# A two-block transformer kernel: masked scores in SBUF, early gate and up products in pairs, other step counts around the second mix

## The chip, the cores and the metric

The kernel runs on one core of a Trainium2 chip. The metric is the device time of one launch in microseconds: 2547.01 us, the median of three runs (2543.77 to 2547.75).

## The reference

Two transformer blocks over 1024 rows of width 1024, all in 32-bit floats. Block one puts 16 meta rows ahead of the sequence, projects, and runs two mixers side by side: a differential attention of 4 heads and a state-space mixer. Block two has a gated spatial mixer and an attention of 8 heads with a forgetting bias. Both end with an output projection ("mix"), norms, and a feed-forward of hidden width 2816.

```python
def probs(qb, k):                                   # block one, per head and block of 128 queries
    s = jnp.einsum('bhqd,bhkd->bhqk', qb, k) * scale
    return jax.nn.softmax(jnp.where(causal, s, -jnp.inf), axis=-1)
attn = probs(q1b, k1) - lam * probs(q2b, k2)
out = jnp.einsum('bhqk,bhkd->bhqd', attn, v32)
...
mix = jnp.einsum('blc,cd->bld', jnp.concatenate([o, y], axis=-1), w_out[l])
h_res = h_res + rms_norm(mix, post_mix_g[l])
h = rms_norm(h_res, pre_ffn_g[l])
f = jax.nn.silu(h @ w_gate) * (h @ w_up)            # written as einsums
h_res = h_res + rms_norm(f @ w_down, post_ffn_g[l])
```

Block two's attention adds differences of a running sum of log gates to the scores and applies the softmax of each half-head by itself.

## The kernel before

**Number format.** A factor of a large product is kept as two rounded tiles, "hi" and "lo" (ScalarE copies into hi, VectorE or GpSimd subtracts for lo), and a product is three matmuls (`mm3`, `mma`: hi*hi, hi*lo, lo*hi). `wpiece` (L99) loads 512 KB of a weight (`wr`, a ring of 2) and splits it into `wh` and `wl`, rings of 4.

**Stages.** The sequence is worked on in two halves of 512 rows. Per block: dense projections, attention of the first half with the other mixer beside it, then `feed_forward` (L1234): the first half's mix (`mix_first`), its norms into H0 (`norm_first`), `up_first` and `down_sums` beside the second half's attention, the second half's mix and norms (`mix_second`, `norm_second`), then `ffn_up` and `ffn_down`, which multiply in a Strassen-like scheme. `up_first` makes those gate and up products that need H0 alone: for each of 11 tiles t of the hidden width one "half" of 24 matmuls for gate and one for up. Within a half, 12 matmuls give a partial product that ScalarE copies out (`p1`, L1038) and SyncE stores; 12 more then accumulate onto the same bank. Gate banks come from a pool of one (`psum_e`), up banks from a pool of two (`psum_d`). ScalarE applies Silu to the gate bank (L1041), VectorE multiplies the up bank in (L1043). `down_sums` (L1008) loads 1 MB of the down weight into a single buffer, forms four sums on GpSimd (L954) and stores them, 11 times.

**Attention.** A step takes one head and 128 queries. For each of the two q/k pairs (block one) or half-heads (block two), `scores` (L630) makes the score product in PSUM (`s`: two banks of 512 columns in the first half, one tile of two banks in the second; in block one, for the last of a half's four query blocks, a further short piece for the 16 meta columns in `t`), lets VectorE add the mask or bias and take the row minimum in one instruction that writes back to PSUM (L649, shown as CUSTOM_DVE_ANT_0 with an accumulator read), and lets ScalarE apply the exponential of each piece from PSUM into P in SBUF with the row sum (L656). Where there are two pieces, VectorE joins minima (L654) and sums (L659). P comes from a ring of four tiles that also holds the k tile of a head (`rowp`). In block one VectorE then combines both P (L754). `transposed_product` (L674) transposes P on TensorE in groups of four 128-column blocks, copies each group out of PSUM alternately on ScalarE (L626) and VectorE (L628), and multiplies with v. At a head's end the normalized output `ob` is stored to DRAM; the second mix loads it as `cat`.

**What sets the order.** The pieces are Python generators that are stepped in turn, which gives program order; a planner then orders every engine's instructions, and SyncE's DMA list, by program order and its own estimates of when inputs are ready. `ahead(n)` moves what is issued under it n instructions forward in priority. `pinned` (L110) ties the first matmul of an early product behind the last score or mix matmul issued before it (`mark`). Engines and SyncE's list run strictly in the order that the planner gave them.

Of the kernel before, what the change touches and what calls it, by code (L numbers as in the profile page):

```python
# [10 lines left out]
F32 = mybir.dt.float32  # L11
F32R = mybir.dt.float32r
I32 = mybir.dt.int32
AF = mybir.ActivationFunctionType
ALU = mybir.AluOpType
# [40 lines left out]
def tile_two_blocks(ctx: ExitStack, tc: tile.TileContext, a, out):  # L56
    nc = tc.nc
    PE, V, S, G, SP = nc.tensor, nc.vector, nc.scalar, nc.gpsimd, nc.sync
# [33 lines left out]
    fD = [dram.tile([7, NT, 128, 512], F32, name=f"fD{i}") for i in range(2)]  # L92
# [167 lines left out]
    def step(gen, n=1):  # L260
        for _ in range(n):
            next(gen, None)

    def ahead(n=500):
        return tc.high_priority(offset=n)
# [28 lines left out]
    with ExitStack() as pre:  # L294
        np_ = pool(pre, "p1n", 3, side="right")
        for rt in range(9):
            n = 128 if rt else NM
# [322 lines left out]

    turn = [0]

    def evac(out_, in_):
        turn[0] += 1
        if turn[0] % 2:
            S.activation(out=out_, in_=in_, func=AF.Copy)  # L626
        else:
            V.tensor_copy(out=out_, in_=in_)  # L628

    def scores(q, k, n, bias, nm, ls, P, fix=None):  # L630

        cuts = ([(0, 1, n)] if n <= 512 else [(0, 1, NM), (NM, 1, 512)] if n <= NH else
                [(0, 2, n // 2)] if n <= 1024 else [(0, 1, NM), (NM, 2, 512)])
        tiles = []
        if len(cuts) > 1:
            m2 = small.tile([128, 2], F32, tag="m2", name="m2")
        for ci, (c0, nb, w) in enumerate(cuts):
            s_ = (psum_s[0] if ci == len(cuts) - 1 else psum_t)()
            s_ = s_.rearrange("p (b c) -> p b c", c=512)
            for b in range(nb):  # L640
                for o in range(2):
                    i = PE.matmul(out=s_[:, b, 0:w], lhsT=q[:, o], rhs=k[:, c0 + b * w:c0 + (b + 1) * w],  # L642
                                  start=o == 0, stop=o == 1)
            sv = s_[:, 0:nb, 0:w]
            if fix is not None:
                dv = s_[:, nb - 1, w - 128:w]
                V.tensor_tensor(out=dv, in0=dv, in1=fix, op=ALU.add)
            bv = bias[:, c0:c0 + nb * w].rearrange("p (b c) -> p b c", b=nb)
            V.tensor_tensor_reduce(out=sv, in0=sv, in1=bv, scale=1.0, scalar=0.0, op0=ALU.add, op1=ALU.min,  # L649
                                   accum_out=m2[:, ci:ci + 1] if len(cuts) > 1 else nm)  # L650
            tiles.append((sv, c0, nb, w))
        mark[0] = i
        if len(cuts) > 1:
            V.tensor_tensor(out=nm, in0=m2[:, 0:1], in1=m2[:, 1:2], op=ALU.min)  # L654
        for ci, (sv, c0, nb, w) in enumerate(tiles):
            S.activation(out=P[:, c0:c0 + nb * w].rearrange("p (b c) -> p b c", b=nb), in_=sv, func=AF.Exp,  # L656
                         scale=-1.0, bias=nm, accum_out=ls[:, ci:ci + 1])
        if len(cuts) > 1:
            V.tensor_tensor(out=ls[:, 0:1], in0=ls[:, 0:1], in1=ls[:, 1:2], op=ALU.add)  # L659

    def split_pair(src, dst, o, eng, other=None):

# [8 lines left out]
                S.activation(out=dst[po, 1 - o, e], in_=src[pi], func=AF.Copy)  # L671
                eng[e].tensor_tensor(out=dst[pi, 1 - o, e], in0=src[pi], in1=hi.bitcast(F32), op=ALU.subtract)

    def transposed_product(bank, out_, P, blocks, last):  # L674

        for b0 in range(0, len(blocks), 4):
            grp = blocks[b0:b0 + 4]
            t = psum_t()
            at = atp.tile([128, 512], F32, tag="at", name="at")
            for b, (c0, w, _) in enumerate(grp):  # L680
                PE.transpose(out=t[0:w, b * 128:(b + 1) * 128], in_=P[:, c0:c0 + w], identity=ident)
            nb = sum(w == 128 for _, w, _ in grp)
            evac(at[:, 0:nb * 128], t[:, 0:nb * 128]) if nb else None
            for b, (c0, w, v) in enumerate(grp):
                if w < 128:
                    evac(at[0:w, b * 128:(b + 1) * 128], t[0:w, b * 128:(b + 1) * 128])
                bank.mm(out_, at[0:w, b * 128:(b + 1) * 128], v, last and b0 + b == len(blocks) - 1)

    def attention(blk, half, side, keep=None):
# [4 lines left out]
        with ExitStack() as ph:  # L694
# [39 lines left out]
            for h in range(4):  # L734
# [7 lines left out]
                for j in range(4):  # L742
                    i = half * 4 + j
                    n = m + (i + 1) * 128
                    P = [rowp.tile([128, nk], F32, tag="row", name="P") for _ in range(2)]
                    for e in range(2):
                        scores(qst[:, :, e, j * 128:(j + 1) * 128], kst[:, e], n,
                               mask[:, nk - n:nk] if blk == 0 else x[:, e, 0:n],
                               nm[:, j, e:e + 1], ls_[:, j, e], P[e], None if blk == 0 else mask)
                    V.reciprocal(out=rl[:, j], in_=ls_[:, j, :, 0])  # L750
                    if blk == 0:
                        V.tensor_scalar(out=cf[:, j:j + 1], in0=rl[:, j, 1:2], scalar1=ls_[:, j, 0, 0:1],
                                        scalar2=nlam[:, 0:1], op0=ALU.mult, op1=ALU.mult)
                        V.scalar_tensor_tensor(out=P[0][:, 0:n], in0=P[1][:, 0:n], scalar=cf[:, j:j + 1],  # L754
                                               in1=P[0][:, 0:n], op0=ALU.mult, op1=ALU.add)
                        blocks = [(NM + b * 128, 128, v[:, b]) for b in range(i + 1)] + [(0, NM, x)]
                        transposed_product(bank, o[:, j * 128:(j + 1) * 128], P[0], blocks, j == 3)
                    else:
                        for e in range(2):
                            es = slice(e * 64, (e + 1) * 64)  # L760
                            transposed_product(bank, o[:, j * 128 + e * 64:j * 128 + (e + 1) * 64], P[e],
                                               [(b * 128, 128, v[:, b, es]) for b in range(i + 1)], j == 3 and e == 1)
                    if j == 1 and h < 3:
                        nxt = load(h + 1)
                    yield
# [257 lines left out]
    def up_first(blk, H0):  # L1023

        sfx = "_2" if blk else ""
        for t in range(NT):
            f11 = rows_out.tile([128, 512], F32, tag="vt", name="f11")
            for g in range(2):
                u = wpiece(a[("w_up" if g else "w_gate") + sfx][t][:, 2:4].rearrange("p b k f -> p (b k f)"))
                bank = (psum_d if g else psum_e)()  # L1030
                for blkn, q in ((1, 0), (0, 1)):
                    for kt in range(4):
                        k0 = blkn * 512 + kt * 128
                        mma(bank, sl(u, slice(None), slice(k0, k0 + 128)), sl(H0, slice(None), 4 * q + kt),
                            q == 0 and kt == 0, q == 0 and kt == 0)
                    if q == 0:
                        s = rows_out.tile([128, 512], F32, tag="vt", name="p1")
                        S.activation(out=s, in_=bank, func=AF.Copy)  # L1038
                        SP.dma_start(out=pD[blk][2 * t + g], in_=s)
                if g == 0:  # L1040
                    S.activation(out=f11, in_=bank, func=AF.Silu)  # L1041
                else:
                    V.tensor_tensor(out=f11, in0=f11, in1=bank, op=ALU.mult)  # L1043
                    SP.dma_start(out=fD[blk][0, t], in_=f11)
                yield

    def ffn_up(blk, A, raws):

# [185 lines left out]
    def feed_forward(blk, att, ffs, fp, mT):  # L1234

        _, _, _, gains = ffn_args(blk)
        with ffs:
# [16 lines left out]
            upf = up_first(blk, H0)  # L1254
            with ExitStack() as th:
                ds = down_sums(blk, pool(th, "utd", 1, side="right"))
                for n in (2, 2, 1, 2, 2, 1, 2, 2, 2):
                    step(att)
                    step(upf, n)
                    step(ds)  # L1260
                drain(ds)
                drain(att)
# [8 lines left out]
            with ExitStack() as mh:  # L1271
                mp = pool(mh, "mx", 2)
                tp = pool(mh, "mxt", 3)
                gp = row_bcast(mp, gains[0], 1024, "ffg0", 1)
                gT = mp.tile([128, KT], F32, name="ffgT", bufs=1)
                SP.dma_start(out=gT, in_=a["ffn_gT_2" if blk else "ffn_gT"])
                ms = mix_second(blk, mp, lambda rt, xt: norm_second(blk, mp, tp, gp, gT, rt, H0, A, F, xt))
                for n in (1, 0, 0, 0, 0, 0, 1):
                    with ahead(400):
                        step(ms)  # L1280
                    step(upf, n)
                for _ in range(2):
                    with ahead(400):
                        step(ms)
                    step(upf, 2)
                drain(ms)
                drain(upf)
            for n, x, q in (("S3", F[0], 0), ("S4", F[1], 1)):
# [316 lines left out]
```

## Time and profile before

| | us |
|---|---|
| median of 3 runs | 2547.01 |
| the profiled execution, its own time | 2551.87 |
| its span in the trace | 2550.2 |
| TensorE busy (share of the span) | 2335.1 (92%) |
| VectorE | 1548.2 (61%) |
| ScalarE | 1131.9 (44%) |
| GpSimd | 869.7 (34%) |
| mean granted TensorE clock | 0.962 |

PE is TensorE's matmul row and PEld its weight loads, DVE is VectorE, ACT ScalarE, POOL GpSimd, SP SyncE (SPq its list of DMAs). Busy time leaves out waiting. The granted clock is the share of full speed; 1.0 is 2.4 GHz. Attention beside other work lies at about 180 to 680 us (block one) and 1400 to 1890 (block two), the second mixes at about 700 to 820 and 1914 to 2030, the large feed-forward products between and after.

### The profile page before, as it was taken

What the parts mean: (1) busy time and instruction counts of PE and PEld (TensorE: products, weight loads), DVE (VectorE), ACT (ScalarE), POOL (GpSimd) and SP (SyncE); (2) the same over time, 40 slices, a digit from 0 to 9 for tenths busy, and PEclk for the clock granted to TensorE, in tenths of its full rate; (3) what the DMA queues carried; (4) which work ended last, traced back from release to release, by engine and by line L of the source; (5) the groups of instructions that cost most, each with busy time, mean ns of one, the idle gap of its engine ahead of it and who ended that gap; (6) DMA issues with size and microseconds to landing.
All of it is one profiled execution on the core that took longest, in us unless ns stands there. A gap on an engine that the chain in (4) does not pass through costs nothing. (4 is left out here: it accounts for less than half of the span.)

```text
span 2550.2 us, 31792 instructions
## 1 busy us (share of the span) xinstructions
PE 2335.1 (92%) x11016; PEld 1891.9 (74%) x11016; DVE 1548.2 (61%) x2485; ACT 1131.9 (44%) x1962; POOL 869.7 (34%) x690
## 2 busy tenths in 40 slices
PE   8997799679698999989999999998979899999997
PEld 6765678567576888868887778877867688887886
DVE  8658764765357667654586446556436776665556
ACT  4334544455354322325454566456535422223543
POOL 1747321134424666620002121113442466661001
PEclk9998989789899999999999999999999999999999
DMA  4432225246764454556666222644676454545666
GB/s 162 145 120 76 72 74 167 90 151 221 259 207 137 159 172 153 173 162 200 196 231 203 80 75 94 224 141 142 226 257 242 150 166 167 169 162 195 207 195 213
DMA packets 201409, 422.83 MB, mean 166 GB/s; under 512 B 33752, under 2 KB 52312, under 8 KB 195104
## 3 DMA queue, kind: packets, MB, share of 16 engines
q1 hardware_dynamic: 201248, 420.79, 49.9%
q8 instruction: 87, 1.43, 0.2%
q14 instruction: 74, 0.61, 0.1%
HBM read 308.78 MB, written 110.76 MB: 165 GB/s over the span
## 5 line engine op out<-in xcount | busy, mean ns | idle before, releaser
L143 POOL TENSOR_TENSOR rs<-rv,mhalf 128x1 f32<-128x1 f32 (+2 forms) x102 | 77.8, 766 | 849.7 <-DVE rv L142 840.6
L105 DVE TENSOR_TENSOR wl<-wr,wh 128x1024 fp32r<-128x1024 f32 x144 | 198.0, 1379 | 172.6 <-ACT wh L104 168.0
L104 ACT ACTIVATE wh<-wr 128x1024 fp32r<-128x1024 f32 x154 | 162.4, 1057 | 201.9 <-DMA wr<-in_w_out 53.0
L180 ACT ACTIVATE uh<-raw 128x512 fp32r<-128x512 f32 x176 | 108.2, 630 | 310.2 <-PE z L949 274.7
L949 PE MATMUL z<-dbl,dah 128*128 128x512 f32 x616 | 240.3, 393 | 5.5 <-DVE dbl L181 5.5
L949 PE MATMUL z<-dbh,dal 128*128 128x512 f32 x616 | 239.5, 391 | 0.0
L949 PE MATMUL z<-dbh,dah 128*128 128x512 f32 x616 | 223.1, 394 | 7.1 <-ACT dbh L180 4.0
L181 DVE TENSOR_TENSOR ul<-raw,uh 128x512 fp32r<-128x512 f32 x176 | 190.5, 1091 | 13.4 <-ACT uh L180 7.0
L181 DVE TENSOR_TENSOR dal<-ra,dah 128x512 fp32r<-128x512 f32 x154 | 108.6, 705 | 135.7 <-ACT dah L180 85.7
L180 ACT ACTIVATE dah<-ra 128x512 fp32r<-128x512 f32 x154 | 97.0, 630 | 197.0 <-DMA ra<-fD 109.4
L642 PE MATMUL s<-kst,qst 128*128 128x512 f32 (+11 forms) x384 | 107.5, 390 | 41.4 <-ACT P L656 37.2
L949 PEld LDWEIGHTS z<-dbh,dah 128*128 128x128 f32 x616 | 116.0, 189 | 35.1 <-ACT dbh L180 6.8
L949 PE MATMUL z<-ffhTh,uh 128*128 128x512 f32 x352 | 137.3, 392 | 5.0 <-DVE s L957 5.0
L949 PEld LDWEIGHTS z<-dbl,dah 128*128 128x128 f32 x616 | 116.1, 189 | 31.9 <-DVE dbl L181 7.9
L656 ACT ACTIVATE P<-s,nm 128x1024 f32<-128x1024 f32 (+13 forms) x128 | 95.2, 744 | 98.5 <-DVE nm L649 95.2
L949 PE MATMUL z<-ffhTl,uh 128*128 128x512 f32 x352 | 137.6, 391 | 0.0
L954 POOL TENSOR_TENSOR raw<-raw 128x512 f32<-128x512 f32 x88 | 136.3, 1569 | 0.0
L949 PE MATMUL z<-ffhTh,ul 128*128 128x512 f32 x352 | 135.8, 391 | 0.0
L127 PEld LDWEIGHTS o<-v,at 128*128 128x128 f32 x864 | 117.4, 205 | 24.6 <-ACT at L626 11.3
L949 PEld LDWEIGHTS z<-dbh,dal 128*128 128x128 f32 x616 | 116.4, 189 | 24.0
L127 PE MATMUL o<-v,at 128*128 128x64 f32 (+1 forms) x864 | 121.6, 288 | 13.0 <-ACT at L626 8.1
L954 POOL TENSOR_TENSOR t<-raw 128x512 f32<-128x512 f32 x44 | 60.0, 1365 | 189.5 <-DMA raw<-in_w_up 97.5
(505 smaller groups left out, 6400.6 us busy)
## 6 DMA issues: line engine op xcount, KB each, us to landing
ra<-fD SPq DMA_DIRECT2D x154, 256.0 KB
wr<-in_w_out SPq DMA_DIRECT2D x48, 512.0 KB
raw<-in_w_gate SPq DMA_DIRECT2D x22, 1024.0 KB
wd<-in_w_down SPq DMA_DIRECT2D x22, 1024.0 KB
fD<-f SPq DMA_DIRECT2D x88, 256.0 KB
raw<-in_w_up SPq DMA_DIRECT2D x22, 1024.0 KB
rb<-tD SPq DMA_DIRECT2D x88, 256.0 KB
tD<-wd SPq DMA_DIRECT2D x66, 256.0 KB
```

Source lines behind the costliest of these rows:

```text
L104: S.activation(out=hi, in_=raw, func=AF.Copy)
L105: (eng or V).tensor_tensor(out=lo, in0=raw, in1=hi.bitcast(F32), op=ALU.subtract)
L127: i = PE.matmul(out=out, lhsT=lhsT, rhs=rhs, start=not self.seen, stop=last).ins
L143: G.tensor_tensor(out=r[:np_], in0=v[:np_], in1=mhalf[:np_, 0:n], op=ALU.pow)
L180: S.activation(out=h, in_=src, func=AF.Copy)
L181: V.tensor_tensor(out=l, in0=src, in1=h.bitcast(F32), op=ALU.subtract)
L642: i = PE.matmul(out=s_[:, b, 0:w], lhsT=q[:, o], rhs=k[:, c0 + b * w:c0 + (b + 1) * w], start=o == 0, stop=o == 1)
L656: S.activation(out=P[:, c0:c0 + nb * w].rearrange("p (b c) -> p b c", b=nb), in_=sv, func=AF.Exp, scale=-1.0, bias=nm, accum_out=ls[:, ci: ...
L949: i = PE.matmul(out=o, lhsT=x, rhs=y, start=first and n == 0, stop=True, skip_group_check=True)
L954: eng.tensor_tensor(out=o, in0=x, in1=y, op=ALU.subtract)
```

## The change

`scores`: the VectorE instruction that adds mask or bias and takes the minimum writes P in SBUF instead of PSUM; one exponential per score row then runs over all of P in place, and the add of two row sums goes away. `evac`: a new argument sends all copies out of PSUM in block one's attention to ScalarE; block two alternates as before. `up_first`: gate and up of a tile are made in one step, both weight pieces first, then 12 gate, 12 up, 12 gate, 12 up matmuls; only the gate's first matmul is pinned. The step counts beside the attention go from 16 halves to 7 pairs; two pairs are issued between the attention's end and the second mix, and two pairs within it (before: six halves within it).

```diff
-    def evac(out_, in_):
+    def evac(out_, in_, act):
         turn[0] += 1
-        if turn[0] % 2:
+        if turn[0] % 2 or act:
             S.activation(out=out_, in_=in_, func=AF.Copy)
         else:
             V.tensor_copy(out=out_, in_=in_)
...
-            V.tensor_tensor_reduce(out=sv, in0=sv, in1=bv, scale=1.0, scalar=0.0, op0=ALU.add, op1=ALU.min,
+            V.tensor_tensor_reduce(out=P[:, c0:c0 + nb * w].rearrange("p (b c) -> p b c", b=nb), in0=sv, in1=bv,
+                                   scale=1.0, scalar=0.0, op0=ALU.add, op1=ALU.min,
                                    accum_out=m2[:, ci:ci + 1] if len(cuts) > 1 else nm)
-            tiles.append((sv, c0, nb, w))
         mark[0] = i
         if len(cuts) > 1:
             V.tensor_tensor(out=nm, in0=m2[:, 0:1], in1=m2[:, 1:2], op=ALU.min)
-        for ci, (sv, c0, nb, w) in enumerate(tiles):
-            S.activation(out=P[:, c0:c0 + nb * w].rearrange("p (b c) -> p b c", b=nb), in_=sv, func=AF.Exp,
-                         scale=-1.0, bias=nm, accum_out=ls[:, ci:ci + 1])
-        if len(cuts) > 1:
-            V.tensor_tensor(out=ls[:, 0:1], in0=ls[:, 0:1], in1=ls[:, 1:2], op=ALU.add)
+        S.activation(out=P[:, 0:n], in_=P[:, 0:n], func=AF.Exp, scale=-1.0, bias=nm, accum_out=ls[:, 0:1])
...
-                        transposed_product(bank, o[:, j * 128:(j + 1) * 128], P[0], blocks, j == 3)
+                        transposed_product(bank, o[:, j * 128:(j + 1) * 128], P[0], blocks, j == 3, True)
...
         for t in range(NT):
-            f11 = rows_out.tile([128, 512], F32, tag="vt", name="f11")
-            for g in range(2):
-                u = wpiece(a[("w_up" if g else "w_gate") + sfx][t][:, 2:4].rearrange("p b k f -> p (b k f)"))
-                bank = (psum_d if g else psum_e)()
-                for blkn, q in ((1, 0), (0, 1)):
+            us = [wpiece(a[n + sfx][t][:, 2:4].rearrange("p b k f -> p (b k f)")) for n in ("w_gate", "w_up")]
+            banks = psum_e(), psum_d()
+            for blkn, q in ((1, 0), (0, 1)):
+                for g, (u, bank) in enumerate(zip(us, banks)):
                     for kt in range(4):
                         k0 = blkn * 512 + kt * 128
                         mma(bank, sl(u, slice(None), slice(k0, k0 + 128)), sl(H0, slice(None), 4 * q + kt),
-                            q == 0 and kt == 0, q == 0 and kt == 0)
+                            q == 0 and kt == 0, q == g == kt == 0)
                     if q == 0:
                         s = rows_out.tile([128, 512], F32, tag="vt", name="p1")
                         S.activation(out=s, in_=bank, func=AF.Copy)
                         SP.dma_start(out=pD[blk][2 * t + g], in_=s)
-                if g == 0:
-                    S.activation(out=f11, in_=bank, func=AF.Silu)
-                else:
-                    V.tensor_tensor(out=f11, in0=f11, in1=bank, op=ALU.mult)
-                    SP.dma_start(out=fD[blk][0, t], in_=f11)
-                yield
+            f11 = rows_out.tile([128, 512], F32, tag="vt", name="f11")
+            S.activation(out=f11, in_=banks[0], func=AF.Silu)
+            V.tensor_tensor(out=f11, in0=f11, in1=banks[1], op=ALU.mult)
+            SP.dma_start(out=fD[blk][0, t], in_=f11)
+            yield
...
-                for n in (2, 2, 1, 2, 2, 1, 2, 2, 2):
+                for n in (1, 1, 1, 0, 1, 1, 1, 0, 1):
                     step(att)
                     step(upf, n)
                     step(ds)
...
-                for n in (1, 0, 0, 0, 0, 0, 1):
+                step(upf, 2)
+                for n in (0, 0, 0, 0, 0, 0, 1, 0, 1):
                     with ahead(400):
                         step(ms)
                     step(upf, n)
-                for _ in range(2):
-                    with ahead(400):
-                        step(ms)
-                    step(upf, 2)
```

## Rows read from the trace of the kernel before

**Rows 1.** The page: busy us of each engine, share of the span, instructions.
```profile
PE 2335.1 (92%) x11016; PEld 1891.9 (74%) x11016; DVE 1548.2 (61%) x2485; ACT 1131.9 (44%) x1962; POOL 869.7 (34%) x690
```

**Rows 2.** Busy time by stretch: from:to, length, busy us (instructions), granted clock, DMA.
```profile
core 0: us, PE busy (x) PEld busy (x) DVE busy (x) ACT busy (x) POOL busy (x), PEclk, DMA share, GB/s
...
180.00:545.00 365.00, 295.49 (x1437) 230.23 (x1436) 248.45 (x510) 181.29 (x385) 119.69 (x105) 0.87 0.30 95
545.00:720.00 175.00, 145.65 (x690) 118.12 (x689) 76.52 (x112) 79.16 (x127) 70.78 (x49) 0.91 0.70 242
720.00:820.00 100.00, 86.50 (x365) 67.61 (x364) 72.78 (x85) 53.59 (x82) 37.42 (x28) 0.95 0.50 171
820.00:1400.00 580.00, 562.87 (x2471) 460.99 (x2470) 374.41 (x493) 225.92 (x372) 201.03 (x146) 0.99 0.55 181
...
1720.00:1920.00 200.00, 167.40 (x940) 143.67 (x939) 89.92 (x151) 100.56 (x150) 81.81 (x60) 0.93 0.62 214
1920.00:2030.00 110.00, 100.28 (x445) 77.96 (x443) 78.56 (x94) 59.32 (x92) 35.18 (x28) 0.98 0.58 199
```

**Rows 3.** TensorE's waits: engine, tile, line, releaser: us in total, times, longest.
```profile
PE s L642 <- ACT P L656: 37.2, 19, 5.5
PE d L949 <- ACT p L1038: 20.6, 9, 8.8
...
PE t L681 <- DVE P L754: 9.9, 6, 4.3
...
PE t L127 <- DVE at L628: 3.6, 1, 3.6
...
PE o L127 <- DVE at L628: 2.5, 3, 1.0
...
PE e L949 <- ACT f L1041: 2.4, 3, 1.8
...
PE e L949 <- ACT p L1038: 1.5, 2, 1.0
```

**Rows 4.** The timeline (start, us, engine, line) around one wait for a score bank.
```profile
521.37 1.23 DVE L649 CUSTOM_DVE_ANT_0 s<-s,mask 128x1024 f32<-128x1024 f32 x1
...
525.59 1.10 ACT L656 ACTIVATE P<-s,nm 128x1024 f32<-128x1024 f32 x1
...
526.84 1.46 PE L642 MATMUL s<-kst,qst 128*128 128x328 f32 x4 [5.51 <-ACT P L656]
```

**Rows 5.** Groups of instructions, 180 to 700 us: xcount | busy, mean ns | idle.
```profile
L626 ACT ACTIVATE at<-t 128x512 f32<-128x512 f32 (+4 forms) x40 | 17.6, 444 | 21.2 <-PE t L681 17.0 <-DVE at L628 3.2 <-PE t L642 0.6
...
L628 DVE COPY at<-t 16x128 f32<-16x128 f32 (+3 forms) x40 | 15.3, 385 | 12.0 <-PE t L681 11.2 <-ACT at L626 0.3
```

**Rows 6.** Silu after a gate product (timeline), and 12 early matmuls (chain).
```profile
1865.07 0.39 PE L949 MATMUL e<-ffhTh,wl 128*128 128x512 f32 x1
1866.34 1.28 ACT L1041 ACT_TABLE_LOAD   x1
1867.64 0.60 ACT L1041 ACTIVATE f<-e 128x512 f32<-128x512 f32 x1
...
1780.81 2.75 PE e L949 x12
```

**Rows 7.** The timeline ahead of block one's second mix.
```profile
683.24 1.06 ACT L104 ACTIVATE wh<-wr 128x1024 fp32r<-128x1024 f32 x1 [8.63 <-DMA wr<-in_w_out]
685.32 0.79 PE L949 MATMUL d<-ffhTh,wh 128*128 128x512 f32 x1 [8.82 <-ACT p L1038]
688.07 0.16 DVE L774 TENSOR_TENSOR rs<-rs,rl 128x4 f32<-128x4 f32 x1 [12.19 <-POOL rs L143]
...
700.21 0.45 PE L172 MATMUL t<-ident,cat 128*128 128x128 f32 x1 [10.21 <-DMA cat<-oD]
```

**Rows 8.** The timeline ahead of block two's second mix.
```profile
1887.85 0.69 DVE L778 TENSOR_TENSOR ob<-o,rl 128x512 f32<-128x512 f32 x1 [1.47 <-PE o L127]
...
1902.38 0.50 SPq L789 DMA_DIRECT2D o2D<-ob  x1
...
1914.01 0.45 PE L172 MATMUL t<-ident,cat 128*128 128x128 f32 x1 [16.46 <-DMA cat<-anD]
```

More of the change, by code (lines that the diff above doesn't have):

```diff
@@ L633, in scores @@
                 [(0, 2, n // 2)] if n <= 1024 else [(0, 1, NM), (NM, 2, 512)])
-        tiles = []
         if len(cuts) > 1:
@@ L672, in split_pair, with transposed_product @@
                 eng[e].tensor_tensor(out=dst[pi, 1 - o, e], in0=src[pi], in1=hi.bitcast(F32), op=ALU.subtract)
-    def transposed_product(bank, out_, P, blocks, last):
+    def transposed_product(bank, out_, P, blocks, last, act):
         for b0 in range(0, len(blocks), 4):
@@ L682, in transposed_product @@
             nb = sum(w == 128 for _, w, _ in grp)
-            evac(at[:, 0:nb * 128], t[:, 0:nb * 128]) if nb else None
+            evac(at[:, 0:nb * 128], t[:, 0:nb * 128], act) if nb else None
             for b, (c0, w, v) in enumerate(grp):
                 if w < 128:
-                    evac(at[0:w, b * 128:(b + 1) * 128], t[0:w, b * 128:(b + 1) * 128])
+                    evac(at[0:w, b * 128:(b + 1) * 128], t[0:w, b * 128:(b + 1) * 128], act)
                 bank.mm(out_, at[0:w, b * 128:(b + 1) * 128], v, last and b0 + b == len(blocks) - 1)
@@ L761, in attention @@
                             transposed_product(bank, o[:, j * 128 + e * 64:j * 128 + (e + 1) * 64], P[e],
-                                               [(b * 128, 128, v[:, b, es]) for b in range(i + 1)], j == 3 and e == 1)
+                                               [(b * 128, 128, v[:, b, es]) for b in range(i + 1)], j == 3 and e == 1, False)
                     if j == 1 and h < 3:
```

## The prediction

> **What bounds the kernel now.** I read the page's busy shares first [rows 1]: TensorE is busy 92% of a 2550.2 us span, no other engine more than 61%. So the time is TensorE's work plus its gaps and what it loses at the lower clock. The next view, the span cut at the stages [rows 2], says where the gaps are. From 820 to 1400 (the feed-forward of the first block) it is busy 562.87 of 580 us; in the two blocks' attention stages it isn't: 180 to 545 has 365 - 295.49 = 69.5 us of gaps at a mean granted clock of 0.87, 545 to 720 has 29.4, 720 to 820 has 13.5, 1720 to 1920 has 32.6. The change touches just these stages, so 145 us of gaps are all that it can win from, and the 2.4 GHz level that is missing where the mean granted clock reads under 1.
>
> The third view, TensorE's waits over the span [rows 3], names what ends the gaps: score products for the exponential (37.2 us in 19 waits), early products for the copy of their first half (20.6), and transposes for the combined P (9.9). The two gaps ahead of the second mix, one in each block, stand in the timeline [rows 7, 8].
>
> **The change part by part.** I count against the profiled execution's own 2551.87 us (span 2550.2 and 1.7 around it); the median of the runs shown, 2547.01, is 4.9 lower, and the forecast is moved by that at the end.
>
> *Scores into SBUF.* Before, a score bank is free for the next product when the exponential has read it. After, when VectorE's minimum has. The timeline of one wait shows the size [rows 4]: TensorE sat 5.51 us until 526.84; the minimum had ended at 522.60 (521.37 + 1.23), the exponential at 526.69. The last 526.7 - 522.6 = 4.1 us go, 74%. Of 37.2 us that is 27.5, the upper end. It won't all stay won: the transposes then wait for the combined P sooner (9.9 us are such waits already), and VectorE, 248 of 365 us busy in the stage with most of these waits, still has to do both minima. The lower end is 0. I take 10, nearer to the lower one, since an earlier score helps only where the rest of the chain isn't what is late.
>
> The instructions themselves: 16 short exponentials on the 16 meta columns leave ScalarE, and 16 adds of the two sums leave VectorE. Both engines run beside TensorE, ScalarE at 44% [rows 1], so this is 0, and where that cover fails a small gain. The exponential's input moves from PSUM to SBUF; no row here has that form, but a plain 128x1024 copy from SBUF takes 1.06 us beside the exponential's 1.10 [rows 4, 7], so between -0.05 and +0.05 each, off the path: 0.
>
> A new wait comes with it: the minimum writes P, so it waits until that buffer is free, a step earlier than the exponential had to. P comes from a ring of four that the transposes and the next head's k tile also hold. Behind the waiting minimum on VectorE stand the splits of the weights, and TensorE waits for those. Price from 0 to the 9.9 us that TensorE waits for P already, once more; taken with the next item.
>
> *Copies out of PSUM in block one all on ScalarE.* 40 copies of 0.385 us (15.3) leave VectorE and become 40 of about 0.444 (17.6) on ScalarE [rows 5]. TensorE's longest waits for VectorE's copies sum to 3.6 + 2.5 = 6.1 us over both blocks [rows 3], the gain's end. On the other side, two copies of a group that ran side by side now run in turn: 16 groups of the half with more than four key blocks by 0.6 us is 9.5 us. With the wait for P: -6 to +19 on the time; I take -1, because VectorE is the busier of the two in 180 to 545 (248 against 181).
>
> *Pairs.* Before, the first 12 matmuls of a product are followed by the copy of the bank and then by 12 more that wait for it. After, 12 matmuls of the other product stand between: 2.75 us [rows 6]. All waits for this copy are 20.6 + 1.5 = 22.1 us; 8.8 of it is one wait that I count with the second mix; the other 13.3 are at most 2.4 us each and go. But the cover of Silu shrinks. There is one gate bank. Before, the whole up product (24 matmuls) stood between the end of a gate product and the next; now its second half, 2.75 us. In [rows 6] the last gate matmul starts at 1865.07 and ends at 1865.46; the table load ends at 1867.62 and Silu at 1868.24, 2.8 us after. So Silu is just covered, and each further us of ScalarE's queue shows. I charge 0.2 us for each of 22 pairs, 4 us, the nearer end of 0 to 22 x 1.8 (the longest wait for Silu today) = 40. Net -9, between -13 and +27.
>
> Here the Trainium skill speaks against the change. The row has the table load at 1.28 us, with the activation starting 0.02 us after it. By "ScalarE: Activation LUTs", section What ACT_TABLE_LOAD costs, a switch of sets costs about 1.28 us and as much again for a drain, some 2.66 in all. By the rows the term is -9; by the Trainium skill each load before a Silu would add 1.4 us to a cover that has nothing left. The trace shows no such second part between the load and the activation, so it disagrees so far as it can show it.
>
> *Two pairs ahead of the second mix, and other counts.* Before, 16 halves run beside the attention, none between its end and the mix, and 6 in it. After it is 7 pairs, 2 pairs, 2 pairs. The stall: in block one TensorE waits 8.82 us at 685.32 and 10.21 at 700.21 [rows 7], in block two 16.46 at 1914.01 [rows 8]; 35.5 in all. Its causes are queues. In block one GpSimd's small power for the last head stands behind the weight sums, VectorE gets it 12.19 us late, and the copy that TensorE waits for stands on ScalarE behind a split that waits 8.63 us for w_out's DMA. In block two the last head is done at 1888.54 but SyncE stores it at 1902.38, behind the stores of the weight sums. None of this is changed. But there is now work for the stall: a pair is 4 x 2.75 = 11.0 us, two are 22. It is the same work as before, so a gain comes only where the place that it left gets shorter: one pair out of the attention loop (83% busy in 545 to 720 and in 1720 to 1920), one out of the mix (87% and 91%) [rows 2]. Between 0 (the mix is late by its own chain and the gaps reappear behind it) and 35.5. I take 5 a block, 10.
>
> SyncE's list moves with it: a pair issues its two weight loads together, its two stores of the first halves and one of the product; the number and bytes are as before, in a stage where the DMA share is 0.70 [rows 2]. GpSimd's list keeps its length. The planner orders everything again by its own costs; I have no row for that and widen the range instead.
>
> *Clock.* In 180 to 545 the mean granted clock is 0.87. If all of the missing 0.13 fell on busy time, it would cost 0.13 x 295 = 38 us [rows 2]. Shorter gaps give a part back: 0 to 19 (half, the share of the waits that could go); I take 2.
>
> Sum: 10 + 1 + 9 + 10 + 2 = 32. 2551.9 - 32 = 2519.9, and less 4.9 for the median: 2515.
>
> **Rivals.**
>
> *Weight slots (slower).* The pieces live in a ring of four split tiles, and the mix's w_out pieces, which the planner puts ahead by 400, take them early: the split at 683.24 already waits 8.63 us for one [rows 7]. A half needs one slot, a pair two at once. Where two or more w_out pieces are held before the two pairs begin, a pair can't be loaded while another runs, and TensorE waits for its load. For: that row, and the pairs stand in program order just there. Against: in the stages without w_out four slots hold two pairs. Price: 4 pairs ahead of the mixes x 8.6 us = 34, and the 10 of the stall not won: 2515 + 34 + 10 = 2559. It decides once these loads cost more than 5.5 us a pair, for the other terms give 22.
>
> *Hidden anyway.* The mix's start is set by the last head's way through GpSimd, SyncE and DRAM, its end by its chain of norms, and attention by VectorE. Then the two pairs only move the gap from before the mix into it, and the score waits come back as waits for P. For: VectorE is busy 72.78 of 100 us in 720 to 820. Against: TensorE is busier than VectorE in each stage. Left are half of the pairs' 9 and half of the scores' 10: 2551.9 - 9.5 - 4.9 = 2537.5.
>
> *Silu too late for the one gate bank.* Each of the 22 pairs is held by 1.2 us, two thirds of the longest wait for Silu now (1.8): 22 x 1.2 = 26 instead of 4, so 2515 + 22 = 2537. For: 2.8 us against 2.75 of cover. Against: three waits for Silu today, 2.4 us together [rows 3]. By the Trainium skill, "ScalarE: Activation LUTs", section What ACT_TABLE_LOAD costs, the drain would hold 22 x 1.4 = 31 instead of 4, an estimate: 2542.
>
> **How the numbers follow.** The forecast gets 0.50 (its own range 2488 to 2536), hidden anyway 0.20, late Silu 0.12, weight slots 0.18. A measurement here tells about 0.2%, 5 us, from no change. Faster than 2542: nearly all of the forecast, 0.65 of hidden anyway, 0.7 of late Silu, a little of the slots: 0.72. Within: 0.10. Slower than 2552: 0.18, nearly all from the slots. Range: 2482 (the scores' and stall's terms at twice what I took are 2495, and 13 for the clock) to 2558 (the slots' case but for its last us).
>
> **What would show it.** Right if the waits of the score products for the exponential are gone and those that replace them are for the minimum, under 15 us in all; if early products wait for the copy of the first half less than 4 us; if the gap before the mix's first transposes is under 8 us a block and 720 to 820 isn't longer. Silu: more than 10 us of waits of the gate bank for it. Slots: waits of early products for the split of a weight piece, near the mixes. Hidden: the same gap, now inside the mix. It is wrong as a whole if 180 to 545 is no shorter, since the largest gaps lie there.

## The result and the profile after

The changed kernel takes 2514.66 us (median of 4 runs, 2511.03 to 2517.69) against 2546.14 us for the kernel before (4 runs, 2543.77 to 2547.75): ratio 0.9877, 95% interval 0.9859 to 0.9894, so 27 to 36 us faster. The profiled execution of the changed kernel takes 2513.14 us, its span is 2511.4; before it was 2551.87 and 2550.2.

The page of the changed kernel, busy us of each engine (share of the span) and instructions:

```profile
PE 2320.9 (92%) x11016; PEld 1887.9 (75%) x11016; DVE 1521.5 (61%) x2429; ACT 1139.6 (45%) x1968; POOL 869.2 (35%) x690
```

The same matmuls are run (11016). What got shorter are TensorE's gaps: 2550.2 - 2335.1 = 215.1 us before, 2511.4 - 2320.9 = 190.5 after, 24.6 of the 38.8 us between the two spans. The other 14.2 us are less busy time, and they can't be put down to the change: a second profiled execution of the changed kernel (span 2523.8, busy 2334.7) has gaps of 189.1 us and as much busy time as before. The stretches, cut at the same times as in [rows 2]:

```profile
180.00:545.00 365.00, 309.72 (x1537) 244.56 (x1536) 246.94 (x481) 196.87 (x410) 130.67 (x113) 0.90 0.34 108
545.00:720.00 175.00, 155.12 (x730) 126.41 (x729) 73.51 (x104) 84.76 (x134) 59.69 (x45) 0.93 0.72 246
720.00:820.00 100.00, 85.72 (x366) 67.71 (x365) 79.33 (x95) 45.73 (x74) 58.04 (x39) 0.95 0.45 155
1720.00:1920.00 200.00, 176.50 (x918) 147.81 (x918) 77.89 (x115) 94.23 (x132) 72.05 (x56) 0.95 0.71 239
```

In 180 to 545 TensorE does 1537 matmul instructions where it did 1437, and the mean granted clock is 0.90 where it was 0.87. Because later stages start sooner, a stretch of fixed times holds other work after than before. Where the time went is read better from the first start of a stage. These are the first products of the early halves (e) and of the large feed-forward (z), of the kernel before:

```profile
L949 PE MATMUL z<-HS1h,uh x176: 387/389/501, 801.1 to 2298.3; 128*128 128x512 f32 x176
L949 PE MATMUL e<-ffhTh,wh x176: 387/392/775, 541.1 to 2007.9; 128*128 128x512 f32 x176
```

and of the changed kernel (ns min/median/max, then first and last start):

```profile
L944 PE MATMUL z<-HS1h,uh x176: 389/389/796, 772.5 to 2260.4; 128*128 128x512 f32 x176
L944 PE MATMUL e<-ffhTh,wh x176: 387/394/795, 522.2 to 1960.3; 128*128 128x512 f32 x176
```

The early products of block one start 18.9 us sooner (541.1, 522.2), the second mix's first transposes 22.1 us sooner (700.2, 678.1), and `ffn_up` 28.6 sooner (801.1, 772.5). Block two: first scores 35.0 us sooner (1396.2, 1361.2), first early product 45.7 (1760.2, 1714.5), second mix 37.3 (1914.0, 1876.7), end 38.8. So 28.6 of the 38.8 us are won in block one, before its `ffn_up`.

In block two the starts mislead. The stretch from the first scores to the first early product is 10.7 us shorter, and the one from there to the mix 8.4 us longer, but the planner moved work from one to the other: TensorE does about 24 matmuls less in the first and about 46 more in the second. Together they are 2.3 us shorter (517.8, 515.5) and hold more early products than before.

TensorE's waits in the changed kernel (us in total, times, longest), against [rows 3]:

```profile
PE t L172 <- DMA cat<-anD: 12.8, 1, 12.8
PE t L172 <- DMA cat<-oD: 11.3, 1, 11.3
...
PE s L641 <- DVE qst L664: 10.0, 4, 5.2
...
PE s L641 <- DVE nm L648: 8.6, 11, 1.4
...
PE t L676 <- DVE P L749: 7.2, 3, 3.5
...
PE d L944 <- ACT wh L104: 5.5, 3, 2.8
PE e L944 <- ACT p L1032: 5.0, 3, 3.2
...
PE s L641 <- DVE qst L667: 4.0, 4, 1.4
...
PE d L944 <- DVE wl L105: 1.7, 3, 0.9
...
PE e L944 <- ACT f L1035: 0.8, 1, 0.8
```

37.2 us of waiting for the exponential are gone, 8.6 us for the minimum have come, and the waits for the combined P did not grow (9.9, now 7.2). Another wait did: score products now wait 16.7 us for the q tile of a head (`qst`: the two lines shown and 2.7 us behind GpSimd), where they waited 4.1 before, among them:

```profile
PE s L642 <- DVE qst L669: 2.7, 1, 2.7
```

All waits of score products together fell from 41.3 to 25.3 us. How a score bank now comes free, in the timeline:

```profile
484.97 1.11 DVE L648 CUSTOM_DVE_ANT_0 P<-s,mask 128x912 f32<-128x912 f32 x1
486.14 1.19 PE L641 MATMUL s<-kst,qst 128*128 128x512 f32 x4 [0.63 <-DVE nm L648]
486.18 1.06 ACT L654 ACTIVATE P<-P,nm 128x912 f32<-128x912 f32 x1 [0.37 <-DVE nm L648]
```

The next score product starts 0.06 us after the minimum's end, before the exponential begins; in [rows 4] it started 0.15 us after the exponential's end. Left over are the two gaps ahead of the mix, 24.1 us together.

### The profile page after: what moved, and what is told of

Same layout as the page of the kernel before. It is cut to its first block, busy times and chain, and to the rows that moved or that the text cites. A ratio compares the mean times of both kernels' runs of the same rounds, so it can differ in the third digit from the quotient of the medians.

```text
span 2511.4 us, 31789 instructions
## 1 busy us (share of the span) xinstructions
PE 2320.9 (92%) x11016; PEld 1887.9 (75%) x11016; DVE 1521.5 (61%) x2429; ACT 1139.6 (45%) x1968; POOL 869.2 (35%) x690
## 4 chain that ended last, share of the span: by engine, by line
PE 39%; DMA 6%; issue 4%; DVE 3%; POOL 3%; ACT 2%; SPq 0%; DVEq 0%; ACTq 0%; POOLq 0%
PE z L944 26%; PE d L116 3%; PE d L117 3%; PE d L118 3%; POOL wd L949 1%; DMA wd<-in_w_down 1%; PE o L127 1%; DMA rb<-in_w_down 1%; DMA ra<-fD 1%; DMA tD<-wd 1%; PE s L641 1%; DVE wl L105 1%; DMA wr<-in_w_out 1%; PE t L676 1%; ACT wh L104 1%
## 5 line engine op out<-in xcount | busy, mean ns | idle before, releaser
L181 DVE TENSOR_TENSOR ul<-raw,uh 128x512 fp32r<-128x512 f32 x176 | 181.1, 1039 | 17.9 <-ACT uh L180 11.9
L654 ACT ACTIVATE P<-P,nm 128x144 f32<-128x144 f32 (+15 forms) x128 | 99.7, 779 | 84.9 <-DVE nm L648 78.1
L127 PE MATMUL o<-v,at 128*128 128x64 f32 (+1 forms) x864 | 115.8, 279 | 15.2 <-issue 6.5
L181 DVE TENSOR_TENSOR dbl<-rb,dbh 128x512 fp32r<-128x512 f32 x154 | 109.3, 710 | 23.3 <-ACT dbh L180 18.7
```

What stands on the lines that cost most here:

```text
L127: i = PE.matmul(out=out, lhsT=lhsT, rhs=rhs, start=not self.seen, stop=last).ins
L181: V.tensor_tensor(out=l, in0=src, in1=h.bitcast(F32), op=ALU.subtract)
L654: S.activation(out=P[:, 0:n], in_=P[:, 0:n], func=AF.Exp, scale=-1.0, bias=nm, accum_out=ls[:, 0:1])
```

## Experiments

Times are compared with runs of the kernel before on the same chip (2554.25 us in the first group of runs, 2553.2 in the second, 2555.57 and 2550.83 later), so the ratios are what counts; microseconds below are (1 - ratio) x the time of before. The changed kernel itself was run beside its variants in the second group alone; the later runs are set against its ratio from there, from other chips. Every edit also makes the planner order the program anew.

### Each part by itself

**Scores in SBUF alone**, added to the kernel before:

```diff
-            V.tensor_tensor_reduce(out=sv, in0=sv, in1=bv, ...
+            V.tensor_tensor_reduce(out=P[:, c0:c0 + nb * w]..., in0=sv, in1=bv, ...
...
-        for ci, (sv, c0, nb, w) in enumerate(tiles):
-            S.activation(out=P[...], in_=sv, func=AF.Exp, ...
+        S.activation(out=P[:, 0:n], in_=P[:, 0:n], func=AF.Exp, ...
```

> The kernel before with only the scores changed: the minimum writes P in SBUF, one exponential in place. By the prediction's sum this term is worth 10 us: some 2536. Rival: the attention stages give nearly the whole gain (of the 38.8 us of span, 18.9 had come in by the first early product and 10.7 between block one's end and block two's first early product), and all of it is the score banks: 2516 to 2522. Second rival: the planner's new order moves any version by 10 us or more, and no part has a price of its own: then this part may lie anywhere, above 2546 too. In the trace the score products' waits for the exponential should be gone under each.

Measured: 2527.2 us, ratio 0.9894 [0.9865, 0.9923], 27 us faster, where the prediction had taken 10 and given 27.5 as the upper end. Score products no longer wait for the exponential; they wait 9.6 us for the minimum and 16.5 for the q tile.

**Pairs alone**: crossed halves, 7 pairs beside the attention, none ahead of the mix, 4 in it.

```diff
-            for g in range(2):
-                u = wpiece(...)
-                bank = (psum_d if g else psum_e)()
-                for blkn, q in ((1, 0), (0, 1)):
+            us = [wpiece(...) for n in ("w_gate", "w_up")]
+            banks = psum_e(), psum_d()
+            for blkn, q in ((1, 0), (0, 1)):
+                for g, (u, bank) in enumerate(zip(us, banks)):
```

> The kernel before with only the pairs: gate and up of a tile in one step, 7 pairs beside the attention, none ahead of the second mix, 4 in it. By the prediction this term is worth 9 us (13 of waits for the copy of the first half, less 4 for Silu): some 2537. Rival, all from the score banks: 2543 to 2548, since the copies' waits are replaced by other waits. The waits of early products for that copy should fall from 22 us to under 6 in each case.

Measured: 2569.93 us, ratio 1.0065 [1.0045, 1.0084], some 16 us slower. TensorE's waits in this run:

```profile
PE s L642 <- ACT P L656: 47.2, 23, 5.5
PE t L172 <- DMA cat<-anD: 26.0, 1, 26.0
PE t L172 <- DMA cat<-oD: 22.5, 1, 22.5
...
PE e L949 <- ACT p L1037: 8.1, 3, 3.9
PE d L949 <- ACT wh L104: 6.6, 2, 5.0
...
PE d L949 <- DVE wl L105: 6.1, 3, 2.8
```

The waits for the copy of the first half fell from 22.1 to 8.1 us, as forecast. But score products wait 10 us more, the mix's transposes 48.5 us where they and the long copy wait took 35.5 [rows 7, 8], and waits for the split of a weight piece appear: 12.7 us, before 2.1.

**Copies on ScalarE alone** (`if turn[0] % 2 or act:`, with `act` true in block one).

> The kernel before with only the copies out of PSUM in block one's attention on ScalarE. By the prediction 1 us: 2545. Rival, VectorE's relief frees the stage up to 545 us (248 of 365 us busy): 2530 to 2538. Second rival, the copies in turn on ScalarE hold TensorE: 2550 to 2556.

Measured: 2545.35 us, ratio 0.9964 [0.9947, 0.9981], 9 us faster. The gain isn't where VectorE is the busier engine: the first early product starts at 541.5, before at 541.1. The second mix starts 4.3 us sooner (695.9) and block two's scores 7.5 (1388.7).

**The two pairs put back into the mix**, all else as changed:

```diff
-                step(upf, 2)
-                for n in (0, 0, 0, 0, 0, 0, 1, 0, 1):
+                for n in (1, 0, 0, 0, 0, 0, 1, 1, 1):
```

> The changed kernel, with the two pairs that stood ahead of the second mix put back into it (one after its first step, then one in each of its last three). By the prediction the two pairs are worth 10 us: 2525. Rival: the gap ahead of the mix stands in the changed kernel too (11.3 us in block one, 12.8 in block two), so the pairs fill nothing: 2512 to 2518.

Measured: 2525.17 us, ratio 0.9882 [0.9851, 0.9912]. The time meets the 2525 expected only because the kernel before takes 2554.25 us in this group, not 2547; by the ratio it is 1 us behind the changed kernel's 0.9877, well within the intervals.

### One part out

The changed kernel again and three with one part undone, on one chip. The changed kernel itself:

> The changed kernel itself, beside its variants on one chip: ratio to before 0.986 to 0.989, the yardstick for the other three.

Measured: 2520.83 us, ratio 0.9872 [0.985, 0.9894]. The two pairs back in the mix, the kernel above once more:

> Once more the changed kernel with the two pairs put back into the second mix, now beside the changed kernel. In the one trace the gap ahead of the mixes is 49.7 us here and 24.1 in the changed kernel, but the mixes begin 9.5 and 3.5 us earlier, and the large up products start 3.4 and 8.8 us later. If the two pairs fill the gap with work that then is missing nowhere, 8 to 11 us slower than the changed kernel (the prediction's 10). If they only move the gap, within 3 us of it.

Measured: 2527.65 us, ratio 0.9891 [0.9873, 0.9909], 5 us behind the changed kernel with overlapping intervals. Its waits ahead of the mix:

```profile
PE t L172 <- DMA cat<-anD: 28.8, 1, 28.8
PE t L172 <- DMA cat<-oD: 19.0, 1, 19.0
```

So the two pairs shorten the gaps from 47.8 to 26.5 us (the changed kernel's run beside it: 15.0 and 11.5), and by the ratios 5 of these 21.3 us are left in the time. With the pairs in the mix (the run in the first group), block one's mix starts at 668.6 after a longer gap and lasts 112.0 us until `ffn_up`; with two of them ahead it starts at 678.1 and lasts 94.4.

The old scores with all else changed (the scores' edit above in reverse):

> The changed kernel with the scores as before (in place in PSUM, two exponentials). By the prediction's term 10 us slower than the changed kernel. Rival, after the scores alone gave 27 us: 25 to 30 us slower, and the pairs, the copies and the two ahead give 5 to 10 together. Third: more than 30, if the pairs (16 us slower by themselves) pay only once the attention beside them is quick.

Measured: 2555.64 us, ratio 1.0006 [0.9993, 1.0019]. The rest of the change gives nothing by itself; beside the rest, the scores are worth (1.0006 - 0.9872) x 2553 = 34 us. The wait for the exponential is back, nearly in full:

```profile
PE s L642 <- ACT P L656: 34.5, 20, 5.5
PE d L949 <- ACT wh L104: 13.6, 2, 11.7
```

Block one's copies alternating again:

> The changed kernel with block one's copies out of PSUM alternating between ScalarE and VectorE again. By the prediction 1 us slower; by the part alone (0.9964, 9 us) 6 to 12 us slower; nothing, if the scores in SBUF have already relieved the stage.

Measured: 2528.02 us, ratio 0.9897 [0.988, 0.9913], 6 us behind the changed kernel, with overlapping intervals. Here the stage in which VectorE is the busier engine does show it: the first early product starts at 529.8, in the changed kernel's run beside it at 522.0.

### What is the early products' new form worth, and what sets the mix's start

**No pairs**: the kernel before with scores and copies alone; halves and counts as before.

> The kernel before with two parts of the change: the scores in SBUF and block one's copies on ScalarE. The early products stay halves in their old places. Theory (the parts add, and the pairs and their places give nothing): 27 us from the scores and 9 from the copies, as each gave alone, so about 2553 - 36 = 2517, ratio 0.986, level with the changed kernel's 0.9872 or a little under it. Rival (the pairs cost 16 us alone only because the score products stalled beside them; with the scores in SBUF they are worth the 9 us of the prediction and the two ahead another 5): 2521 + 14 = 2535, ratio 0.993.

Measured: 2515.24 us, ratio 0.9839 [0.9814, 0.9865], by the ratios 8 us ahead of the changed kernel's 0.9872, with overlapping intervals. The parts add (27 + 9 = 36, measured 41), and the pairs and their places give nothing. The waits that the pairs were to remove are there, 14.6 us, and cost nothing that shows:

```profile
PE t L172 <- DMA cat<-anD: 19.4, 1, 19.4
PE d L944 <- ACT p L1033: 14.6, 5, 4.9
```

**Uncrossed halves in the changed places**, with the counts of the pairs doubled:

```diff
-                for n in (1, 1, 1, 0, 1, 1, 1, 0, 1):
+                for n in (2, 2, 2, 0, 2, 2, 2, 0, 2):
...
-                step(upf, 2)
-                for n in (0, 0, 0, 0, 0, 0, 1, 0, 1):
+                step(upf, 4)
+                for n in (0, 0, 0, 0, 0, 0, 2, 0, 2):
```

> The changed kernel with the products' 12 matmuls back in the old order inside a pair (first half, copy, second half of one product, then the other), in the changed places: 14 halves beside the attention, 4 ahead of the mix, 4 in it. Theory (crossing the halves takes away the waits for the copy of the first half, which were 20.6 us before and are 5.0 after): these waits come back at 13 to 20 us, 2521 + 13 = 2534, ratio 0.9925, and the gap ahead of the mix is as in the changed kernel. Rival (crossing brings nothing on the time, because what the products wait less others wait more): within 4 us of the changed kernel, ratio 0.987.

Measured: 2511.79 us, ratio 0.9827 [0.9798, 0.9856]. Neither case was hit: by the ratios undoing the crossing makes it 11 us faster, and the intervals just overlap. The waits for the copy came to 5.5 us in this order, not 13 to 20.

**Two buffers for the down weights' sums**, in the changed kernel:

```diff
-                ds = down_sums(blk, pool(th, "utd", 1, side="right"))
+                ds = down_sums(blk, pool(th, "utd", 2, side="right"))
```

> The changed kernel with two buffers in place of one for the sums of the down weights. Theory (the chain of 11 sums, 14 us each through one buffer, and their stores in SyncE's list ahead of the last head's set the start of the second mix): the chain ends at least 10 us sooner in each block, the waits of the mix's transposes fall from 24.1 us to under 10, and the time by 10 to 14 us, ratio 0.982. Rival (the start is set by the last head's own way): the waits of the mix's transposes stay at 20 to 24 us and the time within 5 us, ratio 0.985 to 0.989.

Measured: 2476.17 us, ratio 0.9686 [0.9662, 0.971], 47 us under the changed kernel by the ratios (45 by the spans of two profiled executions, 2523.8 and 2478.9), over three times what the theory gave. GpSimd's waits for the next load into the buffer (`wx` for `wd`) fell from 171.8 us in the changed kernel's run of the second group to 60.6.

Block two shows why in SyncE's list of the changed kernel at the end of the attention (start, us, L1015 stores a sum, L784 the last head's output; x is how many):

```profile
1859.28 0.32 SPq L1015 DMA_DIRECT2D tD<-wx  x1
1860.65 2.83 SPq L1015 DMA_DIRECT2D tD<-wd  x3
...
1864.04 0.41 SPq L784 DMA_DIRECT2D o2D<-ob  x1
...
1867.53 1.38 SPq L815 DMA_DIRECT2D cat<-anD  x1
1868.95 0.49 SPq L816 DMA_DIRECT2D cat<-o2D  x1
```

and in VectorE's timeline:

```profile
1846.66 0.68 DVE L773 TENSOR_TENSOR ob<-o,rl 128x512 f32<-128x512 f32 x1
```

The output is done at 1847.34 and stored at 1864.04: 16.7 us in the list behind stores of sums, which in turn wait for GpSimd, which waits for the next load into the one buffer. With two buffers:

```profile
1802.05 0.32 SPq L1015 DMA_DIRECT2D tD<-wx  x1
1803.41 2.80 SPq L1015 DMA_DIRECT2D tD<-wd  x3
1830.64 0.38 SPq L784 DMA_DIRECT2D o2D<-ob  x1
...
1833.84 0.32 SPq L816 DMA_DIRECT2D cat<-o2D  x1
```

The sums are through 24 us before the head is, and its output (done at 1830.61) is stored at 1830.64. A sum takes 9.8 us (first store 1703.97, eleventh 1802.05) where it took 15.5 (1720.05, and 1859.28 for the tenth).

In block one the same task holds another list. There the last head's output waits for a small power on GpSimd, which stands behind a sum that itself waited 8.12 us for its load, until 665.24 (changed kernel: GpSimd, VectorE, SyncE):

```profile
667.83 1.26 POOL L949 TENSOR_TENSOR wd<-wd 128x512 f32<-128x512 f32 x1
669.05 1.01 POOL L143 TENSOR_TENSOR rs<-rv,mhalf 128x4 f32<-128x4 f32 x1
...
670.09 1.22 DVE L769 TENSOR_TENSOR rs<-rs,rl 128x4 f32<-128x4 f32 x1 [8.75 <-POOL rs L143]
...
672.06 0.37 SPq L784 DMA_DIRECT2D oD<-ob  x1
```

VectorE waits 8.75 us for that power; the output is done at 672.03 and stored at once. With two buffers VectorE goes on at 654.96 without such a wait.

TensorE's waits for `cat` are then 2.5 us in all. From the first early product to the mix, in blocks one and two (us, busy, granted clock, DMA share, GB/s), in the changed kernel's run of the second group:

```profile
522.00:678.50 156.50, 136.39 (x661) 0.93 0.72 240
1721.40:1886.00 164.60, 140.42 (x757) 0.95 0.71 234
```

and with two buffers:

```profile
522.10:662.70 140.60, 136.56 (x660) 0.96 0.83 278
1697.50:1839.60 142.10, 135.94 (x746) 0.98 0.82 275
```

So 15.9 + 22.5 = 38.4 of the 44.9 us between the two spans lie ahead of the mixes, and TensorE's gaps there fell from 20.1 + 24.2 to 4.0 + 6.2 us: 34.1 us, of which the waits for `cat` are 24.0 (26.5, then 2.5). The mixes themselves aren't shorter in sum (95.5 and 99.1 us before, 91.9 and 102.6 with two buffers, up to `ffn_up`).

A gap also costs what comes behind it. In the changed kernel's mix of block two (columns as above):

```profile
1857.00:1863.00 6.00, 6.00 (x25) 0.90 0.74 298
1863.00:1877.00 14.00, 1.17 (x6) 0.70 0.98 320
1877.00:1882.00 5.00, 5.00 (x15) 0.50 1.06 402
1882.00:1888.00 6.00, 6.00 (x32) 0.99 1.01 359
```

After 12.8 us without work TensorE runs 5 us at the lower level (granted clock 0.50, 1.2 GHz): 2.5 us lost behind one gap. The planner also ordered the early products and the mix anew with two buffers in sight, and which part of the 47 us is its doing was not separated.

The Trainium skill has this as a best practice ("Trainium Kernel Development and Optimization", section Best Practices): "Double-buffer for performance". The trace agrees, with one thing added: the single buffer's price fell not on the engine that used it (GpSimd, 35% busy) but on what stood behind it in a shared list, a store on SyncE's and a small power on GpSimd's.

**No pairs, two buffers**: scores, copies and the second buffer on the kernel before.

> The kernel before with the scores in SBUF, block one's copies on ScalarE and two buffers for the sums of the down weights; the early products stay halves in their old places. Theory (crossing the halves and putting two pairs ahead of the mix give nothing, with the chain of the sums as without it): level with the changed kernel with two buffers (ratio 0.9686) or some 5 us under it, as without the second buffer (0.9839 against 0.9872), so ratio 0.966 to 0.969. Rival (the crossed halves' gain of 9 us in the prediction was real and only hidden behind the chain of the sums): once the chain is gone the waits for the copy of the first half decide, 14.6 us in the run without pairs against 5.0, and the time is 9 to 14 us above it, ratio 0.972 to 0.974.

Measured: 2471.15 us, ratio 0.9687 [0.9661, 0.9712]: level with the two-buffer version of the changed kernel. Once the chain is out of the way, too, crossed pairs and their places are worth nothing measurable. By the ratios both versions beat the changed kernel by some 47 us; without the pairs the second buffer itself is worth 39 (0.9839 to 0.9687).

## Why the prediction came out right, point by point

The total was right: 2515 forecast, 2514.66 measured. The terms were not; they erred in both directions and cancelled, so that the total fits so closely is luck. Of its own signs, the end of the waits for the exponential, the minimum's waits under 15 us and the shorter stretch up to 545 us came true. The early products still wait 5.0 us for the copy (under 4 was asked), and the gap ahead of the mix missed its sign as well.

- **Scores into SBUF, 10 taken (0 to 27.5): mis-sized.** 27 alone, 34 beside the rest: the upper end and more. The share of one wait that goes (74%) was right: 37.2 us for the exponential gave way to 8.6 for the minimum, 77% less, inside the 15 forecast. The step "It won't all stay won" was right in kind, though the wait that came wasn't the one named: not the transposes' for the combined P (9.9, then 7.2), but 12.6 us more for the q tile. What failed is the choice of a size near the lower end, on the ground that the rest of the chain is what is late. In the run of the scores alone TensorE's gaps fell by 27.2 us (215.1 to 187.9), as much as the time: by 15.9 up to block one's first early product and by 10.1 from there to its mix, where the early products' copies and not the scores had most of the waits. So quicker scores also shortened gaps behind them; by which path isn't shown.
- **Copies on ScalarE, 1 taken (-6 to 19): too small.** 9 us alone, 6 with the rest, inside the bounds. The argument (VectorE is the busier of the two up to 545 us) isn't borne out by the part alone, which leaves that stage as long as it was; beside the new scores it is (7.8 us).
- **Pairs, 9 taken (-27 to 13): wrong sign, though within its bounds.** 16 us slower alone, and level or a few us slower beside the new scores. The waits for the copy did go (22.1 to 5.0; one of those that the prediction put at 2.4 us at most was 4.3, in block two's mix), but they were not what set the end: without pairs they stay at 14.6 us and the time is no worse. Silu, on which the term's cost was put, waits only 0.8 us. In the run of the pairs alone, weight splits (12.7 us), score waits and the gap ahead of the mix grew instead.
- **Two pairs ahead of the mix, 10 taken (0 to 35.5): half of it, 5, and not told apart from none.** The gap was forecast under 8 us a block and is 11.3 and 12.8. The prediction named both causes, GpSimd's power behind the sums in block one and the last head's store behind their stores in block two, and then took them as given ("None of this is changed"); the pairs then fill the place at which that chain is waited for, and the work is missing in the mix.
- **Clock, 2 taken: not shown.** The mean over the span went from 0.962 to 0.965 in the two profiled executions, but in the second group, on one chip, the changed kernel has 0.957 to 0.961 and the kernel before 0.956 to 0.963. In 180 to 545 it did rise, from 0.87 to 0.90 (0.89 in the second group).

Of the rivals, **weight slots** (2559) did not decide: waits for splits in the early products are 5.5 + 1.7 us, before 2.1, against the 34 that it charged. But its mechanism exists; the pairs alone show 12.7 us. **Late Silu**: 0.8 us, no case. By the prediction's estimate from the Trainium skill ("ScalarE: Activation LUTs", section What ACT_TABLE_LOAD costs) the drain would have held the pairs 31 us. The trace speaks against it: in block one of the changed kernel ScalarE's instruction before ends at 586.17, a Silu's table load runs from 586.18 for 1.28 us, and the Silu starts at 587.48, 0.02 us behind it. **Hidden anyway** (2537.5) is right that pairs and places give next to nothing, but not for the reason that the chain of the sums hides them: with the chain out of the way they still give nothing (0.9687 without, 0.9686 with). It is wrong for the scores.

What stays open: why the pairs alone cost as much as 16 us, since their waits show where time is lost but each run also has its own order from the planner; and what the pairs cost beside the new scores, as the intervals allow 0 to some 15 us. Differences of up to 11 us between versions here may be no more than another order by the planner; the 27 and 34 us of the scores and the 39 and 47 of the second buffer are beyond that.

## What to carry to other kernels

A wait that a bank's last reader causes can be worth nearly its full length (here 37 us of waits, 27 won by this edit alone): let the first reader move the data on. A gap that is the end of a chain of loads and stores isn't cured by moving work into it (21 us of gap filled, about 5 won): follow the late transfer back through its queue to the instruction that holds the queue, here a store, and a small power on GpSimd, behind a single-buffered side task, and free that. When several parts of a change are summed, a total that comes out right proves none of the terms; test the parts.

## What the runs showed that was not expected

- An exponential reading SBUF in place takes about as long as one from PSUM: 0.84 us against 0.81 for 128x656, 1.06 against 1.02 for 128x912; 1.16 for 128x1040 in one piece, where before it took 1.10 and 0.27 for 1024 and 16 columns.
- The side task of the sums, 11 a block on the least busy of the four engines, was worth more than the whole change: 47 us (39 without the pairs) against 32.
